# Early loads on ScalarE's queue, a shorter row scale and earlier quarter sums in a one-core hybrid decoder layer

## The chip, the core and the metric

The kernel runs on one core of a Trainium2 chip. The metric is device time in microseconds (us) of one execution. Three runs of the kernel before took 1051.25, 1051.29 and 1051.93 us; the median is 1051.29. The engines are TensorE (PE, with its weight loads as PEld), VectorE (DVE), ScalarE (ACT), GpSimd (POOL) and SyncE (SP), which issues all DMA transfers of the kernel before.

## The reference

One decoder layer on 512 rows of 1024 float32 numbers:

```python
u = rmsnorm(x, ln1_g)
proj = u @ w_in                       # q, k, v, pool_in, z, xbc, dt_raw, gate_pre
y_a = dilated_attention_mixer(q, k, v, rel_bias) @ w_a
y_b = pool_mixer(pool_in, pool_w, pool_scale) @ w_b
y_c = ssd_mixer(z, xbc, dt_raw, ...) @ w_c
gates = sigmoid(gate_pre + b_gate).reshape(b, s, 3, D)
merged = gates[:,:,0] * y_a + gates[:,:,1] * y_b + gates[:,:,2] * y_c
x = x + merged @ w_o
x = x + conv_ffn(rmsnorm(x, ln2_g), ...)
return rmsnorm(x, final_g)

def rmsnorm(x, g):
    return x * rsqrt(mean(x * x, axis=-1) + 1e-6) * g
```

The matrices are x (512 x 1024), w_in (1024 x 10,256), w_a, w_b, w_c, w_o, and the two of the feed-forward part, whose inner width is 2816.

## The kernel before

**Products.** Every float32 product is made of three fast ones. A weight matrix is cast to a high part (`wh`, by ACT, L191) and the rest is its low part (`wl` = raw - wh, by DVE, L211); activations have the same two parts (`uh`, `ul`). `mm3` (L224) adds wh x uh, then wh x ul, then wl x uh (in the order of its loop) into one PSUM bank, with k running over blocks of 128 rows of the inner dimension.

**Jobs and preparation.** The program is a list of jobs (`program`, L1395), each with a piece of weights of up to 1 MB. Ahead of job n the loop at L1581 prepares: the low part of job n+1 (with `job.then`, a difference of weights, behind it), the cast of job n+2 and the load of job n+3 (`prepare`, L1588). Then the body of job n issues its matmuls. Instructions stand on each engine in the order in which the program text issues them; each engine works them off in order, and waits for what an instruction needs.

**Steps.** Smaller work is written as generators. `step()` (L145) is called behind most chunks of matmuls; it issues the casts that were put off (`flush`), then lets every running item go on by one `yield`, in the order in which they were started, and starts one waiting item. `after(n, it)` (L160) lets n steps go by first.

**The start.** Four blocks of 128 rows of x are loaded as two halves of 128 x 512 each (`load_x`, L1457). SP issues block 0, the norm weights `g8`, the identity `eye`, block 1, then the weights of job 0 in two halves and of job 1 (`fetch`, L170), then blocks 2 and 3. PE meanwhile multiplies ones (`warm_up`). For blocks 0 and 1 the loop at L1526 makes the row scale r = 1/sqrt(mean + eps): squares of the two halves with their sums (`squares`, L429: ACT for the first half, DVE or ACT for the second), their sum (L1485), v (L417), a square root on ACT (L418), a reciprocal and one Newton step (L419 to L426). L1528 multiplies the identity by r into `diag`, and PE turns and scales the block in one product (`turn_scale`, L1523). Then ACT casts the weights of job 0 (L1534), and `turned` (L1491) multiplies by the norm weights `g1` and splits into uh (ACT, L1494) and ul (DVE, L1495). The first matmuls on them are at L1507. Ahead of all this ACT loads its table for the square root with a one-element operation on `warm` (L1450).

**The middle.** The v projections of attention groups 1 and 2 are one product of 1024 rows by 768 columns, made with seven quarter products instead of eight (`sevens`, L336, called by `v_pair`, L591). Its jobs come in the order A11, j=4, A12, j=1, j=2, j=3, A22. Those with a number use added or subtracted halves of u, which four items make ahead of time, one for each pair of k (`sums_of_u`, L395). An item takes four steps: A adds uh and ul to plain halves (L400, twice); B makes the sums and differences (L318 to L321); C casts them (ACT, L324, L325); D makes the low parts sal and sbl (DVE, L327, L328). The four items are started by a `Call` ahead of the fourth job of the w_b product:

```python
if i == 3:
    yield Call(lambda: running.extend(after(p + 1, sums_of_u(p)) for p in range(4)))
```

Between that place and the first of the seven jobs lie that job, of two columns of which the first (column 6) has a step in its middle (`chunk_a2`, L239, by `more`), and two gate jobs of two columns each, with a step behind each column. The evacuation of a gate column is a sigmoid on ACT (L1050) and a multiplication on DVE (L1052). Each of the seven jobs has 24 matmuls of 384 columns, 12 for each of two row blocks, and one step at its end; each row block has four with wh x the high parts, four with wh x the low parts, four with wl x the high parts.

**The end.** The last product adds into the rows block by block; behind each block the final norm (`norm_late`, L460) makes the second half of the row, then the first (L473, two operations), and SP stores them in this order (L1383).

Tiles of 128 x 512 come from one pool of 54 (`T`, L108).

Of the kernel before, what the change touches and what calls it, by code (L numbers as in the profile page):

```python
# [10 lines left out]
F32 = mybir.dt.float32  # L11
F32R = mybir.dt.float32r
AF = mybir.ActivationFunctionType
OP = mybir.AluOpType
AX = mybir.AxisListType

P = 128
S = 512
D = 1024
KD = D // P  # L20
EPS = 1e-6
# [62 lines left out]
def trunk(ctx: ExitStack, tc, out, x, rel_bias, ln1_g, w_in, b_gate, w_a, pool_w, pool_scale, w_b,  # L84
# [3 lines left out]
    act, dve, pool, pe, sp = nc.scalar, nc.vector, nc.gpsimd, nc.tensor, nc.sync  # L88

    x, w_in, w_a, w_b, w_c, w_o = x[0], w_in[0], w_a[0], w_b[0], w_c[0], w_o[0]  # L90
    w_up, w_down = ffn_w_up[0], ffn_w_down[0]
    out = out[0]

    cpool = ctx.enter_context(tc.tile_pool(name="const", bufs=1))
# [13 lines left out]
    def T(name, dt=F32, shape=(P, S)):  # L108
        return big.tile(list(shape), dt, name=name, tag="t")
# [7 lines left out]
    def small(name, shape, dt=F32):  # L117
        return tiny.tile(list(shape), dt, name=name, tag="tiny")

    eye = cpool.tile([P, P], F32, name="eye")  # L120
# [4 lines left out]
    waiting, running = [], []  # L125
    FREE = ()

    def fill(items):

        for it in items:  # L130
            at = next((i for i, w in enumerate(waiting) if w is FREE), None)
            if at is None:
                waiting.append(it)
            else:
                waiting[at] = it
# [24 lines left out]
    def after(n, it):  # L160
        for _ in range(n):
            yield
        yield from it
# [57 lines left out]
    def wsrc(w, k0, k1, c0, c1):  # L221
        return w[k0 * P:k1 * P, c0:c1].rearrange("(k p) c -> p k c", p=P)
# [91 lines left out]
    def sums_of(f0, f1, ah, al, found):  # L314


        sa, sb = T("sa"), T("sb")
        dve.tensor_tensor(sa[:, LO], f0[:, HI], f1[:, HI], OP.add)  # L318
        dve.tensor_tensor(sa[:, HI], sa[:, LO], f0[:, LO], OP.subtract)
        dve.tensor_tensor(sb[:, LO], f0[:, LO], f0[:, HI], OP.subtract)  # L320
        dve.tensor_tensor(sb[:, HI], f1[:, LO], sa[:, HI], OP.subtract)  # L321
        yield
        bh, bl = T("sbh", F32R), T("sbl", F32R)
        act.copy(ah, sa)  # L324
        act.copy(bh, sb)  # L325
        yield
        dve.tensor_sub(al, sa, ah.bitcast(F32))  # L327
        dve.tensor_sub(bl, sb, bh.bitcast(F32))  # L328
        for j, h, l, half in ((1, ah, al, LO), (2, ah, al, HI), (3, bh, bl, LO), (4, bh, bl, HI)):
            found(j, h[:, half], l[:, half])  # L330
# [64 lines left out]
    def sums_of_u(p):  # L395

        f = []
        for k in (2 * p, 2 * p + 1):
            f.append(T("uf"))
            dve.tensor_tensor(f[-1], uh[:, k, :].bitcast(F32), ul[:, k, :].bitcast(F32), OP.add)  # L400
        yield
        yield from sums_of(*f, T("sah", F32R), T("sal", F32R),
                           lambda j, h, l: US.__setitem__((j, p), (h, l)))
# [10 lines left out]
    def rstd_of(ss, cols, n):  # L414

        sq, v, r, t, r2 = (small(nme, [P, cols]) for nme in ("sq", "v", "r", "rt", "r2"))
        dve.tensor_scalar(v, ss, 1.0 / n, EPS, OP.mult, OP.add)  # L417
        act.activation(sq, v, AF.Sqrt)  # L418
        dve.reciprocal(r, sq)  # L419
        if cols == 1:  # L420
            dve.scalar_tensor_tensor(t, r, v, r, OP.mult, OP.mult)
        else:
            dve.tensor_mul(t, r, r)
            dve.tensor_mul(t, t, v)
        dve.tensor_scalar(t, t, -0.5, 1.5, OP.mult, OP.add)
        dve.tensor_mul(r2, t, r)  # L426
        return r2

    def squares(eng, src, ss):  # L429
        junk = T("junk")  # L430
        if eng is act:
            act.activation(junk, src, AF.Square, accum_out=ss)
        else:
            dve.scalar_tensor_tensor(junk, src, 1.0, src, OP.mult, OP.mult, accum_out=ss)
# [933 lines left out]
    def early(tb):  # L1368
        yield
        fin[tb] = norm_early(X1[tb, 0], fin["g"])  # L1370

    def blocks_of(h, acc, opened, keep):
        def evac(tb, ps):
            t = X1[tb, h]
            dve.tensor_tensor(t, t, ps, OP.add)
            if h == 0:
                running.append(early(tb))
                return
            v0, xg0 = fin[tb]
            for _ in norm_late(t, fin["g"], v0, lambda xg1: ((xg1, xg1), (xg0, xg0))):  # L1380
                xg1 = _
            for i, o in ((1, xg1), (0, xg0)):
                sp.dma_start(out[tb * P:(tb + 1) * P, i * S:(i + 1) * S], o)  # L1383

        return jobs_b(lambda k0, k1: [wsrc(w_down, KS + k0, KS + k1, h * S, h * S + S)], S,
                      lambda k, tb: ACTS[KS + k][0][:, tb * P:(tb + 1) * P],
                      lambda k, tb: ACTS[KS + k][1][:, tb * P:(tb + 1) * P], KF - KS, evac,
                      mk=(MM, SM)[h], tail=2 if h else 0, acc=acc, opened=opened, keep=keep)
# [6 lines left out]
    def program():  # L1395
        yield from jobs_a(w_in, C_POOL, 8, uhk, ulk, KD, pool_evac)
        yield Call(lambda: waiting.append(rows_of_bias()))
        yield from v_jobs(0)
        yield from qk_jobs(0)
        yield from pool_out_job()  # L1400
        yield Call(lambda: attend(0))
        yield Call(lambda: waiting.insert(3, ssd_prep()))
        for i, job in enumerate(branch_jobs(1, w_b, YB, 8, more=range(7))):
            if i == 3:
                yield Call(lambda: running.extend(after(p + 1, sums_of_u(p)) for p in range(4)))
            yield job
        load, pair = v_pair()
        yield Call(load)
        yield from gate_jobs(1, 0, SPLIT)
        yield from pair  # L1410
        yield from qk_jobs(1)
        yield Call(lambda: attend(1))
        yield from gate_jobs(1, SPLIT)
        yield from jobs_a(w_in, C_XBC, 12, uhk, ulk, KD, xbc_evac)
        yield Call(ssd_start)
        yield from qk_jobs(2)
        yield Call(lambda: attend(2))
        yield Call(lambda: fill([after(2, combine())]))
        yield from gate_jobs(0)
        many = {"a": branch_jobs(0, w_a, AO, 3), "g": gate_jobs(2),  # L1420
                "Z": z_jobs(0), "z": z_jobs(1)}
        for token in MIX:
            if token in many:
                yield next(many[token])
            else:
                yield Call(lambda i=int(token): waiting.append(y_norm(i)))
        yield Call(finish)
        yield from branch_jobs(2, w_c, YT, 8, last=True)
        yield Call(load_x1)
        for pair in range(2):  # L1430
            for h in range(2):
                yield from wo_jobs(pair, h)
            if pair == 0:
                yield Call(ff_cols)
        for i, job in enumerate(up_jobs()):
            yield job
            if i == 3:
                yield Call(put_x1)
        yield Call(lambda: fin.setdefault("g", grow(final_g)))
        yield Call(finish)  # L1440
        yield from down()

    jobs = list(program())
    weights = [j for j in jobs if isinstance(j, Job)]


    xin, warm = {}, small("warm", [P, 1])
    dve.memset(ones, 1.0)
    dve.memset(warm, 1.0)
    act.activation(warm, warm, AF.Sqrt)  # L1450
# [3 lines left out]
        for i in range(n):  # L1454
            pe.matmul(first[3][:, :P], ones, ones, start=True, stop=True)

    def load_x(tb):  # L1457
        for h in range(2):
            t = xin[tb, h] = T("xin")
            sp.dma_start(t, x[tb * P:(tb + 1) * P, h * S:(h + 1) * S])  # L1460

    load_x(0)
    g8, g1 = T("g8"), cpool.tile([P, KD], F32, name="g1")
    sp.dma_start(g8[:KD, :P], ln1_g[0].rearrange("(k p) -> k p", p=P))
    sp.dma_start(eye, c_eye)
    load_x(1)
    fetch(weights[0], 2)
    fetch(weights[1])
    load_x(2)
# [10 lines left out]
    def row_squares(tb, ss, n=1, eng=dve):  # L1480

        for i in range(n):
            squares(act, xin[tb + i, 0], ss[:, i:i + 1])
            squares(eng, xin[tb + i, 1], ss[:, n + i:n + i + 1])
        dve.tensor_tensor(ss[:, :n], ss[:, :n], ss[:, n:2 * n], OP.add)  # L1485
        return ss[:, :n]
# [30 lines left out]
    diag = [T("diag") for _ in range(2)]  # L1517
# [6 lines left out]
        pe.matmul(bank(k)[:, tb * P:(tb + 1) * P], x_block(tb, k), diag[tb][:, :P], start=True, stop=True)  # L1524

    for tb in range(2):  # L1526
        r = rstd_of(row_squares(tb, small("ss", [P, 2]), eng=(dve, act)[tb]), 1, D)
        dve.tensor_scalar(diag[tb][:, :P], eye, r, None, OP.mult)  # L1528
        if tb == 0:
            for k in range(KD):  # L1530
                turn_scale(0, k)
# [12 lines left out]
    ss = row_squares(2, small("ss", [P, 4]), 2)  # L1544
    next(parts)
    r = rstd_of(ss, 2, D)
    for tb in (2, 3):
        for h in range(2):
            t = xin[tb, h]
# [30 lines left out]
    n = 0  # L1580
# [66 lines left out]
```

## Time and profile before

| | us |
|---|---|
| runs (median, lowest, highest) | 1051.29, 1051.25, 1051.93 |
| profiled execution, its own time | 1052.9 |
| span of the profiled execution | 1050.8 |
| PE busy | 1037.0 |
| DVE busy | 642.9 |
| ACT busy | 467.4 |
| first matmul on uh (L1507) | 13.32 |
| first matmul of the job A11 | 209.55 |
| last matmul's result taken (L1375) | 1043.98 |
| last store issued | 1047.6 |

Times inside an execution count from the start of its span. A line of the profile's timeline gives start, length, engine, line of the code, operation and its tiles, and in brackets the idle time before and what ended it. The list of waits gives who waited for whom: total, times and longest. The chain is followed back from the last instruction, at each step to what released it. The table by windows gives, for each stretch, the busy time of the engines, the clock that TensorE was granted (1.00 is full), the share of the 16 DMA engines and the rate in GB/s. A busy PE can be a waiting one or a slow one in part, since matmuls are pipelined and the clock can be lower; so the granted clock is read beside it.

### The profile page before, as it was taken

The numbers are of one execution on the slowest core, as the hardware profiler recorded it, in microseconds if no ns is written. First come the engines' busy times: TensorE is split into PE (matmuls) and PEld (weight loads), VectorE is DVE, ScalarE is ACT, GpSimd is POOL, SyncE is SP. The second block draws the span as 40 slices with busy tenths as digits, with TensorE's granted clock in tenths as the row PEclk, the third lists the DMA queues.
The fourth block names the chain that finished last, engine by engine and source line by source line (L and its number), as shares of the span: only waits on it lengthen the run. The fifth ranks groups of instructions, "written<-read, shape, count | busy, mean of one in ns | idle before, by whom it ended". The sixth has DMA issues, their size and how long they took to land.

```text
span 1050.8 us, 13095 instructions
## 1 busy us (share of the span) xinstructions
PE 1037.0 (99%) x5220; PEld 864.9 (82%) x5220; DVE 642.9 (61%) x867; ACT 467.4 (44%) x753; POOL 137.7 (13%) x118
## 2 busy tenths in 40 slices
PE   8999999999999999999999999999999999999997
PEld 8888877898888887787887888898888888878885
DVE  5563565675356657576658856766766556556545
ACT  5432544343474363566554324545444443433331
POOL 1670000000000001100143500001111111110110
PEclk9999999999999999999999999999999999999999
DMA  7544312026322354641252426653232322362322
GB/s 241 156 125 136 113 49 74 31 56 182 104 80 81 80 149 112 151 121 52 79 147 85 150 91 220 205 161 119 81 119 82 107 94 82 119 240 67 114 100 80
DMA packets 119787, 121.80 MB, mean 116 GB/s; under 512 B 5523, under 2 KB 101590, under 8 KB 119727
## 3 DMA queue, kind: packets, MB, share of 16 engines
q1 hardware_dynamic: 119727, 120.98, 37.4%
q8 instruction: 41, 0.67, 0.3%
q14 instruction: 19, 0.16, 0.0%
HBM read 115.07 MB, written 4.32 MB: 114 GB/s over the span
## 4 chain that ended last, share of the span: by engine, by line
PE 94%; DVE 3%; DMA 1%; ACT 1%; issue 1%; POOL 0%; SPq 0%; DVEq 0%; ACTq 0%; POOLq 0%
PE pa L230 32%; PE pu L230 22%; PE pb L230 17%; PE pqk L230 9%; PE pa L1507 2%; PE p L230 2%; PE ps L656 1%; PE pu L1329 1%; PE po L695 1%; PE pt L683 1%; PE ppw L230 1%; DVE wl L211 1%; PE py L955 1%; DMA raw<-in_w_in_dram 1%; PE pyo L961 1%
## 5 line engine op out<-in xcount | busy, mean ns | idle before, releaser
L211 DVE TENSOR_TENSOR wl<-raw,wh 128x2048 fp32r<-128x2048 f32 (+3 forms) x95 | 218.6, 2302 | 80.3 <-ACT wh L191 42.3
L191 ACT CAST wh<-raw 128x1024 fp32r<-128x1024 f32 (+3 forms) x188 | 189.6, 1026 | 68.5 <-DVE raw L333 21.1
L230 PE MATMUL pa<-uh,wh 128*128 128x512 f32 x384 | 98.8, 399 | 0.0
L1165 DVE SCALAR_TENSOR_TENSOR hc<-pu,fcol,hc 128x510 f32<-128x510 f32 x88 | 65.9, 748 | 50.8 <-ACT hc L1162 49.2
L230 PE MATMUL pa<-uh,wl 128*128 128x512 f32 x384 | 95.0, 390 | 0.3 <-DVE wl L211 0.3
L230 PE MATMUL pa<-ul,wh 128*128 128x512 f32 x384 | 95.0, 390 | 0.0
L230 PEld LDWEIGHTS pa<-uh,wl 128*128 128x128 f32 x384 | 72.0, 188 | 15.6 <-DVE wl L211 0.7
L230 PEld LDWEIGHTS pa<-ul,wh 128*128 128x128 f32 x384 | 72.1, 188 | 15.2
L230 PE MATMUL pu<-uh,wh 128*128 128x512 f32 (+1 forms) x352 | 83.7, 380 | 0.0
L230 PE MATMUL pu<-uh,wl 128*128 128x512 f32 (+1 forms) x352 | 83.5, 380 | 0.0
L230 PE MATMUL pu<-ul,wh 128*128 128x512 f32 (+1 forms) x352 | 83.5, 380 | 0.0
L230 PEld LDWEIGHTS pa<-uh,wh 128*128 128x128 f32 x384 | 70.2, 188 | 15.2 <-issue 1.0
L230 PEld LDWEIGHTS pu<-uh,wh 128*128 128x128 f32 x352 | 64.1, 188 | 12.7 <-ACT uh L448 0.2
L230 PEld LDWEIGHTS pu<-ul,wh 128*128 128x128 f32 x352 | 64.2, 188 | 12.5
L230 PEld LDWEIGHTS pu<-uh,wl 128*128 128x128 f32 x352 | 64.2, 188 | 12.5
L1162 ACT ACTIVATE hc<-pu,fcol,fcol 128x512 f32<-128x512 f32 x40 | 31.2, 779 | 75.4 <-PE pu L230 75.2
L1170 POOL TENSOR_TENSOR hc<-hc 128x512 f32<-128x512 f32 x22 | 31.5, 1430 | 223.5 <-DVE hc L1165 169.3
L934 POOL TENSOR_TENSOR xd<-xc,dec 128x512 f32<-128x512 f32 x6 | 6.4, 1063 | 364.0 <-DVE xc L925 345.4
L677 ACT ACTIVATE sb<-sb,nm 128x128 f32<-128x128 f32 (+1 forms) x72 | 30.1, 419 | 22.9 <-DVE nm L674 17.2
L1050 ACT ACTIVATE sg<-pa,col 128x512 f32<-128x512 f32 x24 | 16.5, 687 | 51.8 <-PE pa L230 51.7
L230 PE MATMUL pqk<-uh,wh 128*128 128x512 f32 x144 | 36.9, 394 | 0.0
L230 PE MATMUL pqk<-ul,wh 128*128 128x512 f32 x144 | 36.3, 390 | 0.0
(343 smaller groups left out, 1752.4 us busy)
## 6 DMA issues: line engine op xcount, KB each, us to landing
raw<-in_w_in_dram SPq DMA_DIRECT2D x25, 1024.0 KB
raw<-in_ffn_w_up_dram SPq DMA_DIRECT2D x22, 1024.0 KB
raw<-in_w_in_dram SPq DMA_DIRECT2D x20, 512.0 KB
raw<-in_ffn_w_down_dram SPq DMA_DIRECT2D x10, 1024.0 KB
raw<-in_w_o_dram SPq DMA_DIRECT2D x8, 1024.0 KB
raw<-in_w_b_dram SPq DMA_DIRECT2D x4, 1024.0 KB
al<-ad SPq DMA_DIRECT2D x16, 256.0 KB
raw<-in_w_c_dram SPq DMA_DIRECT2D x4, 1024.0 KB
```

The costliest lines, as they stand in the source:

```text
L191: act.copy(job.high[:, :, o], job.raw[:, :, o])
L211: (eng or dve).tensor_tensor(l[:, :, o], job.raw[:, :, o], h[:, :, o].bitcast(F32), OP.subtract)
L230: pe.matmul(ps, l, r, start=first and n == 0, stop=last and n == total - 1)
L656: pe.matmul(pss[i][:, o:o + w * P], q[r, n * P:(n + 1) * P], k[r, kb * P:(kb + w) * P], start=True, stop=True)
L677: act.activation(sb[:, off:off + w * P], sb[:, off:off + w * P], AF.Exp, bias=nm[:, n, h:h + 1], accum_out=ls[:, n, h:h + 1])
L683: pe.transpose(pt[:, o:o + P], sb[:, o:o + P], eye)
L695: pe.matmul(po[DH * hh:DH * hh + DH, n * P:(n + 1) * P], V[g, kb + i][:, (2 * c + hh) * DH:(2 * c + hh + 1) * DH], probs[2 * c + hh, nb][: ...
L1050: act.activation(s, ps, AF.Sigmoid, bias=col[:, o:o + 1])
L1162: act.activation(t, ps, AF.Identity, bias=ff["c1"][:, ff["b"] + m:ff["b"] + m + 1], scale=fw(2, m))
L1165: dve.scalar_tensor_tensor(t[:, sh:], ps[:, :S - sh], fw(k, m), t[:, sh:], OP.mult, OP.add)
L1170: pool.tensor_tensor(a, a, t, OP.mult)
L1507: pe.matmul(first[2 * n + j][:, lo:hi], a[:, k, j * P:(j + 1) * P], b[:, k, lo:hi], start=a is wh and b is uh and k == 0, stop=a is wl and ...
```

## The change

There are four edits.

1. The loads of block 1 of x, of the identity and of the norm weights are issued by ACT, and stand at the head of ACT's program, before the operation on `warm`. SP's order is block 0, the weights of jobs 0 and 1, blocks 2 and 3.
2. The row scale of blocks 0 and 1 is written out in place: the two sums of squares have tiles of their own and go into v one after the other, and `diag` is the identity times r times the Newton factor rt in one operation, so that the product of the two is no longer made.
3. The four items of added halves wait p steps instead of p + 1.
4. Of the last row block (tb = 3) the first half of the row is stored by ACT instead of SP.

```diff
-                sp.dma_start(out[tb * P:(tb + 1) * P, i * S:(i + 1) * S], o)
+                (sp if i or tb < 3 else act).dma_start(out[tb * P:(tb + 1) * P, i * S:(i + 1) * S], o)
...
-                yield Call(lambda: running.extend(after(p + 1, sums_of_u(p)) for p in range(4)))
+                yield Call(lambda: running.extend(after(p, sums_of_u(p)) for p in range(4)))
...
+    def load_x(tb, eng=sp):
+        for h in range(2):
+            t = xin[tb, h] = T("xin")
+            eng.dma_start(t, x[tb * P:(tb + 1) * P, h * S:(h + 1) * S])
+
+    g8, g1 = T("g8"), cpool.tile([P, KD], F32, name="g1")
+    load_x(0)
+    load_x(1, act)
+    act.dma_start(eye, c_eye)
+    act.dma_start(g8[:KD, :P], ln1_g[0].rearrange("(k p) -> k p", p=P))
     dve.memset(ones, 1.0)
     dve.memset(warm, 1.0)
     act.activation(warm, warm, AF.Sqrt)
...
-    load_x(0)
-    g8, g1 = T("g8"), cpool.tile([P, KD], F32, name="g1")
-    sp.dma_start(g8[:KD, :P], ln1_g[0].rearrange("(k p) -> k p", p=P))
-    sp.dma_start(eye, c_eye)
-    load_x(1)
     fetch(weights[0], 2)
     fetch(weights[1])
     load_x(2)
...
-        r = rstd_of(row_squares(tb, small("ss", [P, 2]), eng=(dve, act)[tb]), 1, D)
-        dve.tensor_scalar(diag[tb][:, :P], eye, r, None, OP.mult)
+        s0, s1, v, sq, r, rt = (small(n, [P, 1]) for n in ("s0", "s1", "v", "sq", "r", "rt"))
+        squares(act, xin[tb, 0], s0)
+        squares((dve, act)[tb], xin[tb, 1], s1)
+        dve.tensor_scalar(v, s0, 1.0 / D, EPS, OP.mult, OP.add)
+        dve.scalar_tensor_tensor(v, s1, 1.0 / D, v, OP.mult, OP.add)
+        act.activation(sq, v, AF.Sqrt)
+        dve.reciprocal(r, sq)
+        dve.scalar_tensor_tensor(rt, r, v, r, OP.mult, OP.mult)
+        dve.tensor_scalar(rt, rt, -0.5, 1.5, OP.mult, OP.add)
+        dve.tensor_scalar(diag[tb][:, :P], eye, r, rt, OP.mult, OP.mult)
```

## The prediction

> **What bounds the kernel now.** First the page: busy shares and the slices with the granted clock.
>
> ```profile
> PE 1037.0 (99%) x5220; PEld 864.9 (82%) x5220; DVE 642.9 (61%) x867; ACT 467.4 (44%) x753; POOL 137.7 (13%) x118
> PEclk9999999999999999999999999999999999999999
> ```
>
> TensorE (PE) is busy 99% of the span. So a change can gain only where PE waits or runs at a lower clock: at the start, in the few waits that are left, and behind the last matmul. The list of PE's waits is the second view (total, times, longest in us); its other four lines sum to 2.3 us.
>
> ```profile
> PE uT L1524 <- DVE diag L1528: 2.2, 2, 1.5
> PE pb L230 <- DVE sbl L328: 2.2, 1, 2.2
> ```
>
> The change touches the first two and the tail. Third, the chain that ended last, in order of time, shows which of them is paid for.
>
> ```profile
> 3.88 7.94 DMA raw<-in_w_in_dram
> 11.87 0.93 issue
> 12.80 0.48 ACT uh L1494
> ...
> 214.37 1.67 DVE w L333
> 216.04 0.60 DVE sal L327
> 216.64 0.61 DVE sbl L328
> 217.25 0.04 issue
> 217.29 25.59 PE pb L230 x137
> ```
>
> At the start the chain runs not through diag (L1528) but through the transfer of the first weights: their second half is issued at 3.88 and lands at 11.82, ACT casts it, and only then comes uh. In the middle it leaves PE for 3.3 us of VectorE (DVE): a difference of weights (L333) and the two subtractions of the last halves (sal, sbl). The windows around that place (length; PE, PEld, DVE, ACT, POOL busy; granted clock; DMA share; GB/s) show a second loss.
>
> ```profile
> 213.56:217.29 3.73, 1.55 (x9) 1.23 (x8) 3.73 (x5) 1.94 (x3) 0.00 (x0) 1.00 0.00 0
> 217.80:221.00 3.20, 3.20 (x12) 3.20 (x11) 2.78 (x2) 0.48 (x1) 0.00 (x0) 0.50 0.00 0
> 221.75:225.90 4.15, 4.15 (x25) 4.15 (x25) 1.75 (x2) 3.42 (x5) 0.00 (x0) 1.00 0.00 0
> ```
>
> PE stands for 2.2 us, and behind that its clock is 0.50 from 217.8 to 221; the stretch behind that has 1.00 again.
>
> **The added halves one step sooner (the middle).** Each of four items takes four steps: A (two additions, L400), B (four half-wide operations, L318 to L321), C (two casts on ACT), D (two subtractions, L327 and L328). Item 3 has its D in the eighth step behind the line that starts them: three steps in the last job of w_b (column 6 of `more` has one in the middle), four in the two gate jobs, and the eighth behind the first of the seven jobs ("A11"). The second of the seven (j=4) reads sbl of all items. So D of item 3 is queued behind that job's low part (L211) and the difference W0 (L333). With after(p) it falls in the seventh step, ahead of both.
>
> Price of the stall: the 24 matmuls of job j=4 take from 213.56 to 221.75 (starts of weight loads) = 8.19 us; the next 24 of the same shape take 221.75 to 225.91 = 4.16. Difference 4.0 us: 2.2 of standing, 1.8 of half clock.
>
> Does DVE manage it? From 199.59 to 212.62 it has no pause: three multiplications of yo (L1052) 1.8, D 1.2, B 1.46, A 1.2, low part 1.8, difference 1.7, D 1.2, B 1.47, D 1.2: 13.0 us. One D, one B and one A (3.9 us) of these go a step ahead, where DVE has pauses of 4.17 us before 192.33 and 2.72 before 199.59 (behind 192.33 it then has 0.6 + 1.2 + 1.46 + 1.2 + 1.3 = 5.8 us, done at 198.1). In the new order 8.6 us follow 199.59, done at 208.2. Next is the multiplication that waits for ACT's sigmoid (209.75 + 0.69 = 210.44): 0.65 to 211.1, D of item 3 1.2 to 212.3, the low part 1.75 to 214.05. Job j=4 starts at 213.56 and needs sbl of item 3 at its eighth matmul (214.8) and the low part at its ninth (213.56 + 8 x 0.173 = 214.95). Both are there, the tighter by 0.9 us. What is late next: the low part for A12 ends at about 217.6 and is needed at 219.1. Later work hangs on PE's own progress, so it moves along. I take **-4.0**; bounds -2.2 (the half clock stays) and -4.1.
>
> A rule to weigh here: the Trainium skill (TensorE: Matmul & The Clock Gate, "Part 1: The HAM clock gate") gives half rate after at least one idle window of about 3.4 us. A stand of 2.2 us would not bring it by that, and the middle would then be worth 2.2; the rows show the half clock right behind 2.2 us.
>
> **Loads by ScalarE's queue (the start).** SP issues in this order now; each line is start and length, and the third has three transfers.
>
> ```profile
> 0.74 0.86 SPq L1460 DMA_DIRECT2D xin<-in_x_dram  x2
> 1.65 0.37 SPq L1464 DMA_DIRECT2D g<-in_ln_g_dram  x1
> 2.06 0.35 SPq L1465 DMA_DIRECT2D eye<-in_c_eye_dram  x1
> 2.46 0.90 SPq L1460 DMA_DIRECT2D xin<-in_x_dram  x2
> 3.40 4.83 SPq L179 DMA_DIRECT2D raw<-in_w_in_dram  x3
> ```
>
> Four issues leave SP, so the first weights are issued at 1.65 instead of 3.40. But until their second half lands, the same engines move the same bytes: 0.52 MB for each of two blocks, 1.05 MB of weights, 0.07 of identity and norm weights, 2.17 MB. They are at work from 2.0 on, with one dip (the last two columns are DMA share and GB/s):
>
> ```profile
> 2.00:3.50 1.50, 1.50 (x9) 1.50 (x8) 0.00 (x0) 0.22 (x2) 0.00 (x0) 1.00 0.94 303
> 3.50:4.50 1.00, 1.00 (x7) 1.00 (x6) 0.01 (x1) 0.65 (x2) 0.00 (x0) 1.00 0.83 179
> 4.50:8.00 3.50, 2.84 (x18) 2.65 (x18) 1.99 (x9) 1.00 (x4) 0.00 (x0) 1.00 0.92 284
> ```
>
> At about 300 GB/s the microsecond from 3.5 would move 0.30 MB and moved 0.18: 0.12 MB / 300 GB/s = 0.4 us. That is what an earlier issue can fill. I take **-0.4**; the bounds are -1.75 (the full 3.40 - 1.65) and +1.8 (below).
>
> What it adds: four issues on ACT ahead of its table load. No issue by ACT is in this trace; by SP's rows one takes 0.27 (a tiny one) to 3.69 us (the weights behind a full queue), and one of x at most 1.61. By the nearest rows, SP's own at an empty queue, it is 0.41 with the gap: ACT's load of 1.28 us then starts at 2.4 instead of 0.73 and its Sqrt of warm ends at 3.9, where ACT idles until 3.85 anyway. Cover: behind its last issue ACT needs table load 1.28, warm 0.2, squares 0.8, wait for v and Sqrt 0.85, two squares 1.65, Sqrt 0.6, two casts 2.0 = 7.4 us to uh. With uh at 12.4 the last issue may end at 4.9, 1.04 us each. At 1.61 each it ends at 7.2 and uh comes at 14.6: +1.8.
>
> Block 0 now shares the engines with block 1. Its halves landed at 3.85 and 4.49; both blocks together (1.05 MB at 300 GB/s from 2.0, and the lag of 1 to 2 us behind the bytes that x shows) land by 6.5 to 7.5, block 1 (8.29 before) sooner. Identity lands with them and is needed for diag. Then diag of block 0 is done near 8.1 (7.04 before) and diag of block 1 at 10.2 (10.77 before); the weights at 11.4 still come last. PE would stand from the end of its warm-up (6.43) to 8.2; its stand of 1.5 us before 10.83 left the clock at 1.00, that of 2.2 in the middle did not. At half clock the 16 turns of block 0 take 4.1 instead of 2.05 us, to 12.3, and uh comes at about 12.8, the whole gain of the start.
>
> **The scale.** For each block the product L426 (0.16) goes, and the sum L1485 becomes a second v operation of the same size: one operation less a block. In block 1 one v operation also runs before the second sum is ready. Off that chain go 0.19 + 0.2 = 0.4 us. It lies beside the transfer of the weights: **0**. Uncovered it would be a gain of 0.4.
>
> **The last store by ACT.** The last stores on SP:
>
> ```profile
> 1047.17 0.81 SPq L1383 DMA_DIRECT2D out_dram<-xg  x2
> ```
>
> The second issue starts at 1047.6, and DVE has the second half (L473, 1046.59 + 1.00) at 1047.59, so SP is not what it waits for: **0**, bounds -0.35 (one issue) and +0.45 (a dearer one on ACT).
>
> **Sum.** -4.0 - 0.4 = -4.4 us. The profiled execution took 1052.9 (span 1050.8 and 2.1 around it); it would take 1048.5. It lies 1.6 above the median of 1051.29, whose runs have no profile. On the median: **1046.9 us**. A measurement tells 0.2% (2.1 us) from no change.
>
> **Rivals.**
> - *The middle gives only part* (0.13): DVE is over 0.9 us later than worked out, or the half clock comes without the stand. For it: the margin is thin, and DVE's order is full. Against: the pauses ahead are 6.9 us for 3.9. -0.4 - 2.2: **1048.7**.
> - *The start gives nothing or loses* (0.16): the engines have the same 2.17 MB to move, at a share of 0.8 to 1.1 already, and PE's stand or ACT's issues may cost. -4.0 + 0 = **1047.3**; with issues of 1.61 us 1051.29 - 4.0 + 1.8 = **1049.1**. Beside it stands the Trainium skill (DMA: Bandwidth & Descriptors, "Issuing engines are not separate DMA queues"): transfers of all engines run on the same 16 DMA engines, and only time to issue is saved. By that rule it is 1047.3; the share in the rows agrees but for the dip.
> - *The stall only moves* (0.07): item 3 is in time, but its operations push a low part past its need, and PE stands as long at A12 or at j=1. Against: margins of 1.5 and 1.4 us there. Only the start's 0.4 is left: **1050.9**.
> - *Slower* (0.04): ACT's four issues hold its table load. With 3.69 us each the last ends at 15.5 and uh comes at 22.9, +10.1; less 4.0: **1057.4**. It decides from 2.7 us an issue, where the start loses 6.1. Against: the 3.69 was behind a full queue.
>
> The forecast has 0.60, on its own 1045.3 to 1047.8. The range: down to 1045.3 (start -1.75, middle -4.1, end -0.1), up to 1049.2, the first two rivals within. Below 1049.2 lies faster: 0.60 + 0.13 + 0.16 = 0.89, of which 0.01 goes to the same: 0.88; same 0.08; slower 0.04.
>
> **What would show it.** Right: no wait of PE for sbl, the job j=4 in about 4.2 us, clock 1.00 through it; first weights landed near 11.4 and uh near 12.4; ACT's first square before 4.6; the tail as long as now. Wrong: a wait of PE for wl between 213 and 226, a clock of 0.5 there without a stand, uh later than 12.8, or issues on ACT over 1 us.

## The result, and the profile after

| | before | after |
|---|---|---|
| median of 20 runs each (us) | 1051.21 | 1049.24 |
| lowest, highest | 1048.74, 1053.35 | 1046.47, 1051.41 |
| profiled execution, its span | 1052.9, 1050.8 | 1049.47, 1047.4 |
| first square of block 0's second half (L434) | 4.49 | 6.42 |
| `diag` of block 0, of block 1 | 6.75, 10.49 | 8.29, 9.95 |
| first matmul on uh (L1507 before, L1508 after) | 13.32 | 14.18 |

The ratio is 0.998, with a 95% interval of 0.9972 to 0.9988: 1.3 to 2.9 us faster. That is a little under half of the forecast gain of 4.4 us. 1049.24 lies just above the upper end of the range (1049.2), and the gain lies on the 0.2% that a measurement tells from no change, with the interval on both sides of it. The two profiled executions differ by 3.4 us, more than the medians; so what follows is read from places inside the executions, each over several of them.

First the list of PE's waits in the kernel after (total, times, longest; all of it).

```profile
PE uT L1525 <- DVE v L1531: 2.2, 1, 2.2
PE pa L1466 <- DVE relb L511: 1.1, 1, 1.1
PE pb L230 <- DVE wl L211: 0.5, 1, 0.5
PE pu L230 <- ACT uh L448: 0.2, 1, 0.2
```

The wait for sbl (2.2 us) is gone. A wait of the same length has come at the start, for the turning of block 0. The line names v, but that is the v of block 1, the next operation on DVE (8.55 to 8.70). What PE needed is `diag`, to which the weight load of the same products is put down, and the chain, in order of time, runs through it (first the weight load from the timeline, then the chain):

```profile
8.69 2.42 PEld L1525 LDWEIGHTS uT<-diag,xin 128*128 128x128 f32 x16 [2.45 <-DVE diag L1537]
```

```profile
1.19 5.21 DMA xin<-in_x_dram
6.40 0.02 issue
6.42 0.70 DVE junk L434 x2
...
8.29 0.35 DVE diag L1537
8.64 0.07 DVE v L1531
8.71 2.69 PE uT L1525 x16
11.40 0.20 PE pa L1541
11.61 2.81 PE uT L1525 x16
14.42 9.59 PE pa L1508 x80
```

The chain starts with a transfer of x that lands at 6.40, the second half of block 0, and no longer with the weights. Then it runs through the scale, `diag`, and the turns of both blocks. Each 16 turns take 2.7 to 2.9 us; in the kernel before they took 2.05. The windows (length; PE, PEld, DVE, ACT, POOL busy; granted clock; DMA share; GB/s) tell why, and what the transfers did:

```profile
2.00:3.50 1.50, 1.50 (x9) 1.50 (x8) 0.00 (x0) 0.61 (x1) 0.00 (x0) 1.00 0.90 195
3.50:4.50 1.00, 1.00 (x7) 1.00 (x6) 0.00 (x0) 0.87 (x2) 0.00 (x0) 1.00 0.83 238
4.50:8.00 3.50, 2.04 (x10) 1.74 (x9) 1.24 (x6) 1.31 (x4) 0.00 (x0) 1.00 1.10 333
...
10.00:12.70 2.70, 2.70 (x13) 2.45 (x13) 0.46 (x2) 1.25 (x2) 2.42 (x2) 0.50 1.09 347
213.00:217.80 4.80, 4.80 (x30) 4.80 (x29) 4.59 (x4) 2.52 (x5) 0.00 (x0) 1.00 0.00 0
217.80:221.00 3.20, 3.20 (x20) 3.20 (x20) 2.47 (x3) 2.15 (x4) 0.00 (x0) 1.00 0.00 0
```

Behind the stand at the start the clock is 0.50 from 10.0 to 12.7; in windows of 0.1 us the half clock reaches from 9.9 to 13.3, which is 3.4 us. In the middle it is 1.00 throughout, without a stand. From 2.0 to 8.0 the engines move 0.29 + 0.24 + 1.17 = 1.70 MB, against 0.45 + 0.18 + 0.99 = 1.62 MB in the profiled execution before: hardly more. What changed is which bytes go first. The timeline (start, length, engine; in brackets the idle time before and what ended it):

```profile
0.74 0.90 ACTq L1452 DMA_DIRECT2D xin<-in_x_dram  x2
0.74 0.87 SPq L1452 DMA_DIRECT2D xin<-in_x_dram  x2
1.66 5.09 SPq L179 DMA_DIRECT2D raw<-in_w_in_dram  x3
1.66 0.45 ACTq L1457 DMA_DIRECT2D eye<-in_c_eye_dram  x1
2.15 0.71 ACTq L1458 DMA_DIRECT2D g<-in_ln_g_dram  x1
2.89 1.28 ACT L1461 ACT_TABLE_LOAD   x1 [2.89 <-issue]
...
6.42 0.69 DVE L434 SCALAR_TENSOR_TENSOR junk<-xin 128x512 f32<-128x512 f32 x1 [5.39 <-DMA xin<-in_x_dram]
...
10.67 1.04 ACT L191 CAST wh<-raw 128x1024 fp32r<-128x1024 f32 x1 [0.47 <-DMA raw<-in_w_in_dram]
```

Block 1 is issued by ACT at the same time as block 0 by SP, and the weights follow at 1.66. ACT's four issues take 0.41 to 0.71 us each, and its table load ends at 4.17, ahead of the first data. The second half of the weights is taken at 10.67, which is earlier than before (11.85). ACT still waited 0.47 us for it, but the first matmul no longer does.

**Where the time went, by places.** Two matmuls that every kernel has cut the execution into stretches: the first at L656 (attention scores) and the first at L955. The middle lies between them, the start ahead of them.

| | before | after | difference |
|---|---|---|---|
| start to first L656 | 126.2 | 127.0 | +0.8 |
| first L656 to first L955 | 274.3 | 270.3 | -4.0 |
| last L1375 to the end of the span | 6.8 | 6.9 | +0.1 |

The rest (L955 to the last L1375) takes 642.2 to 644.4 us in all executions of all kernels below. It varies without regard to the edits, and it is why one execution, or a difference of two spans, doesn't settle a gain of 2 us.

### The profile page after: what moved, and what is told of

Same layout as the page of the kernel before. It is cut to its first block, busy times and chain, and to the rows that moved or that the text cites. A ratio compares the mean times of both kernels' runs of the same rounds, so it can differ in the third digit from the quotient of the medians.

```text
span 1047.4 us, 13090 instructions
## 1 busy us (share of the span) xinstructions
PE 1036.3 (99%) x5220; PEld 864.5 (83%) x5220; DVE 642.6 (61%) x865; ACT 467.6 (45%) x753; POOL 138.0 (13%) x118
## 4 chain that ended last, share of the span: by engine, by line
PE 92%; DVE 3%; DMA 2%; ACT 2%; issue 0%; DVEq 0%; SPq 0%; ACTq 0%
PE pa L230 35%; PE pu L230 22%; PE pb L230 13%; PE pqk L230 9%; PE pa L1508 2%; PE p L230 2%; DVE wl L211 2%; PE ps L656 1%; PE po L695 1%; PE pt L683 1%; DMA raw<-in_ffn_w_up_dram 1%; PE ppw L230 1%; ACT wh L191 1%; PE py L955 1%; DMA raw<-in_w_o_dram 1%; PE pyo L961 1%
## 5 line engine op out<-in xcount | busy, mean ns | idle before, releaser
L230 PEld LDWEIGHTS pu<-uh,wh 128*128 128x128 f32 x352 | 64.1, 188 | 12.8 <-ACT uh L448 0.4
```

Source lines behind the costliest of these rows:

```text
L230: pe.matmul(ps, l, r, start=first and n == 0, stop=last and n == total - 1)
```

## The experiments

**The order of arrival** is the theory. The middle gives its whole 4.0 us. The start loses 1.6 us of that, because one queue on SP delivered in the order of need (block 0, identity, block 1, weights), while two queues share the same engines: block 0 lands late, PE stands for over 2 us and then turns at half clock. It has three rivals. **The clock:** in the middle the half clock comes by chance or anyway, only the stand of 2.2 us is gained, and the start is neutral. **The issues:** ACT's four issues hold its table load and its squares. **The small edits:** the short scale or the last store costs something.

The expectations are quoted as they were recorded ahead of each run. Where letters stand in them for the theories of that moment, the numbers beside the letters are what the run is held against. The times came above what was expected by 0.4 to 0.5 us in e3, e6, e7, e8 and e9, and by 1.7 us in e10; the first matmul on uh came later than expected in e5, e7, e9 and e10.

The starts of all kernels in one table, so that each run can be looked up: DVE's square of block 0's second half; `diag` of block 0 and of block 1; ACT's cast of the second half of the weights ("ready": it did not wait for the transfer); first matmul on uh; first L656; whether the clock was 0.50 in the turns.

| kernel | square | diag 0 | diag 1 | weights | on uh | L656 | half clock |
|---|---|---|---|---|---|---|---|
| before | 4.49 | 6.75 | 10.49 | 11.85 | 13.32 | 126.2 | no |
| b0_before_again | 4.39 | 6.65 | 8.87 | 10.26 | 11.73 | 124.7 | no |
| e1_sums_alone | 4.54 | 6.8 | 9.3 | 10.63 | 12.10 | 125.0 | no |
| e12_sums_again | 4.50 | 6.77 | 9.34 | 10.83 | 12.30 | 125.2 | no |
| e8_no_act_loads | 4.13 | 6.00 | 8.95 | 11.24 | 12.71 | 125.6 | no |
| e6_block_1_on_sp | 4.75 | 6.62 | 8.28 | 10.29 | 11.76 | 124.7 | no |
| after | 6.42 | 8.29 | 9.95 | 10.67 | 14.18 | 127.0 | yes |
| e2_start_alone | 5.75 | 8.12 | 9.70 | ready | 14.01 | 126.8 | yes |
| e11_changed_again | 5.63 | 7.92 | 9.50 | ready | 13.80 | 126.6 | yes |
| e3_longer_warm_up | 5.71 | 8.48 | 10.06 | ready | 12.82 | 125.6 | no |
| e5_identity_first | 4.64 | 6.51 | 10.54 | ready | 14.30 | 127.2 | yes |
| e7_identity_first_filled | 4.64 | 6.51 | 11.04 | ready | 13.25 | 126.0 | no |
| e9_both_blocks_on_act | 6.41 | 8.28 | 11.89 | ready | 15.32 | 128.1 | yes |
| e10_halves_over_both_queues | 4.94 | 6.82 | 9.37 | 12.13 | 13.61 | 126.5 | no |

### The change taken apart

**The kernel before once more** has no edit.

> The kernel before, unchanged, for the clock of each of its executions. Its profiled execution has 1.6 us of lost clock behind the stand for sbl (half clock from 217.8 to 221.2) and about 1.6 behind the last matmul: 0.997. Theory C (the half clock behind a stand of about 2 us comes in some executions only, and for lengths that differ): the mean clock spreads over 0.995 to 0.999 and the time follows it, near 1 us for 0.001. Rival S (it comes in each execution alike): all at 0.997, and the times spread for another reason.

Measured: 1050.97 us, ratio 1.0001 (0.9993 to 1.001). The middle stretch is 274.3 us again. The wait and the window around it (columns as above) are those of the first execution:

```profile
PE pb L230 <- DVE sbl L328: 2.2, 1, 2.2
```

```profile
217.20:220.50 3.30, 3.30 (x12) 3.30 (x11) 1.82 (x2) 0.21 (x1) 0.00 (x0) 0.50 0.00 0
```

So the half clock behind the stand in the middle is no accident of one execution. But it does not come in every one. Each run has its mean granted clock on record, and the traces tell how to read it. Every stretch of half clock in them lasts 3.4 us (6.8 in e9), and each 3.4 us take 0.0016 off the mean; behind the last matmul every trace loses some more. The seven traces with such a stretch at the start or in the middle have means of 0.995 to 0.997, the seven without one 0.998 or 0.999. All runs sorted by that (number of runs, mean time):

| kernel | 0.997 or less | 0.998 or more |
|---|---|---|
| before (b0 and the runs beside the experiments) | 48, 1051.8 us | 46, 1050.4 us |
| after (result and e11) | 21, 1049.6 us | 11, 1047.7 us |
| halves alone (e1, e12) | 1, 1049.1 us | 13, 1047.4 us |
| longer warm-up (e3) | none | 12, 1048.4 us |

By this the half clock in the middle came in about half of the runs of the kernel before, and the one at the start in two of three runs of the changed kernel; the runs with it are 1.4 and 1.9 us longer. That is theory C of the expectation, and not rival S, which wanted 0.997 in all. It is read from rounded means: these runs have no trace of the stretch itself, and the twelve of b0 alone show the link of clock and time only faintly.

The start differs between the two executions as well. Chain and timeline of this run:

```profile
3.88 6.36 DMA raw<-in_w_in_dram
10.24 0.02 issue
```

```profile
10.26 1.04 ACT L191 CAST wh<-raw 128x1024 fp32r<-128x1024 f32 x1 [0.76 <-DMA raw<-in_w_in_dram]
```

With the same program the second half of the weights landed at 10.24 instead of 11.82. The prediction had taken 11.82 as a property of the kernel; it is one draw of a time that varies by 1.6 us (five executions with these loads: 10.24, 10.6, 10.8, 11.2, 11.8).

**Only the added halves** (kernel before with one edit):

```diff
-  running.extend(after(p + 1, sums_of_u(p)) for p in range(4))
+  running.extend(after(p, sums_of_u(p)) for p in range(4))
```

> Only the added halves one step sooner. Both theories: no wait of PE for sbl, job j=4 in 4.2 us, and the start as before (first matmul on uh at 13.3). Theory C: the gain is the stand of 2.2 us in each execution and 1.8 of half clock in some of them: 2.2 to 4.0 us, near 3, and a mean clock of 0.998 to 0.999 with little spread. Rival S: 4.0 us.

Measured: 1047.47 us, ratio 0.9969 (0.9957 to 0.998). The middle stretch is 270.3 us (125.0 to 395.3), 4.0 less than in all three traced executions with the late halves, and no wait for sbl is left. The half clock goes with the stand; had it come anyway, only 2.2 would be gained, and that half of the rival falls. The other half, that it comes by chance, holds by the clocks above: the three traces had it, and in a run without it only the stand of 2.2 us is there to gain. Over all runs that makes about 3.1 us (an estimate: 2.2 and half of 1.8). The ratio, 3.3 us with an interval of 2.1 to 4.5, does not tell this from 4.0.

**Only the start** (kernel after, with the halves and the store put back):

```diff
-  running.extend(after(p, sums_of_u(p)) for p in range(4))
+  running.extend(after(p + 1, sums_of_u(p)) for p in range(4))
...
-  (sp if i or tb < 3 else act).dma_start(out[...], o)
+  sp.dma_start(out[...], o)
```

> Only the start: loads by ACT's queue and the shorter scale; halves and last store as before. Theory C: block 0 lands 1.9 us later because block 1 shares the engines, PE stands about 2.2 us behind its warm-up, and half clock comes behind that in most executions: slower by 0.7 us (as in the profiled execution of the changed kernel) to 3, near 1. Rival S: slower by 0.7, alike in all. Rival Q (the loss is one of ACT's queue, such as the later table load): PE's first stand is not what decides, and the time stays the same when the stand is filled.

Measured: 1053.05 us, ratio 1.0021 (1.0011 to 1.0032). By itself the new start costs 1.2 to 3.4 us. Middle stretch 274.3, as before. Its chain and its window at the start:

```profile
1.66 6.35 DMA eye<-in_c_eye_dram
...
8.12 0.35 DVE diag L1537
```

```profile
10.00:12.00 2.00, 2.00 (x9) 1.75 (x9) 0.21 (x2) 1.00 (x1) 1.96 (x1) 0.50 1.09 349
```

Here the last to come was the identity: issued at 1.66 behind block 1 in ACT's queue, landed at 8.02. In the kernel after it was block 0's second half. Both are the same displacement: something that was early in one queue now stands beside or behind half a megabyte of block 1. The half clock is there too.

**The changed kernel with a longer warm-up** (`WARM = 12` to `WARM = 16`, eight matmuls of ones more), to shorten PE's stand.

> The changed kernel with 16 instead of 12 warm-up products, so that PE works until about 8.3 us and stands 0.4 instead of 2.15 before diag. Theory C: the clock stays at 1.00 to 14 us, turns of block 0 in 2.05 us, first matmul on uh at 12.4 to 12.9 instead of 14.2, the mean clock 0.998 to 0.999, and 1.3 to 3 us faster than the changed kernel: 1046.2 to 1048. Rival Q: no gain over the changed kernel (1049.2).

Measured: 1048.37 us, ratio 0.9977 (0.9969 to 0.9985). The eight matmuls made the warm-up only 0.45 us longer (it ends at 6.99 instead of 6.54), so the stand of 0.4 us that was expected did not come. Here `diag` was later still, since it waited for the identity until 8.48, but PE stood for 1.89 us instead of 2.15 and the clock stayed at 1.00 (timeline, then window):

```profile
8.48 0.35 DVE L1537 TENSOR_SCALAR diag<-eye,r,rt 128x128 f32<-128x128 f32 x1 [0.93 <-DMA eye<-in_c_eye_dram]
8.88 2.05 PE L1525 MATMUL uT<-diag,xin 128*128 128x128 f32 x16 [1.89 <-DVE v L1531]
...
12.82 0.72 PE L1508 MATMUL pa<-uh,wh 128*128 128x256 f32 x4
```

```profile
10.00:12.00 2.00, 2.00 (x18) 1.86 (x17) 0.54 (x3) 1.50 (x3) 1.60 (x1) 1.00 1.09 349
```

18 matmuls in the window where e2 has 9. The first matmul on uh comes at 12.82 instead of 13.8 to 14.2. So the loss of the start has two parts: about 1.2 us by the half clock, and about 0.4 us by the late `diag` itself (12.82 against a mean of 12.43 of the five executions with all loads on SP). The times of e3 and after overlap, so the split rests on the traces; the mean clocks agree with it (no run of e3 at 0.997 or less, 21 of the 32 of the changed kernel).

### Which load must come first

**The identity ahead of block 1 on ACT's queue:**

```diff
-  load_x(1, act)
   act.dma_start(eye, c_eye)
   act.dma_start(g8[:KD, :P], ...)
+  load_x(1, act)
```

> The changed kernel, with ACT issuing identity and norm weights ahead of block 1. Theory L (the loads on a second queue share the engines with block 0, and identity comes behind block 1): identity no longer holds diag, but block 0's second half still lands at 5.5 to 6.5 instead of 4.4, so diag of block 0 is done at 7.6 to 8.6, PE stands 1.2 to 2.2 us; a part of the loss stays: first matmul on uh at 12.5 to 14, time 1048 to 1049. Rival I (identity alone is late): diag at 7.0, first matmul at 11.7 to 12.1 as with the loads of before, 1047. Rival A (ACT's late table load holds the first square): first square not before 4.4, and no change against the changed kernel.

Measured: 1048.76 us, ratio 0.9981 (0.9971 to 0.999). Block 0 and the identity are on time again (`diag` at 6.51), but block 1 is not:

```profile
4.64 0.69 DVE L434 SCALAR_TENSOR_TENSOR junk<-xin 128x512 f32<-128x512 f32 x1 [3.61 <-DMA xin<-in_x_dram]
...
7.69 0.63 ACT L432 ACTIVATE junk<-xin 128x512 f32<-128x512 f32 x1 [1.85 <-DMA xin<-in_x_dram]
...
8.72 0.63 ACT L432 ACTIVATE junk<-xin 128x512 f32<-128x512 f32 x1 [0.30 <-DMA xin<-in_x_dram]
```

Its halves, now beside the weights, land at 7.7 and 8.7; in b0 both were squared by 7.3. PE stands twice (1.4 and 1.8 us), the turns of block 1 run at half clock in this trace, and nothing is won: the stand has moved from block 0 to block 1. By the mean clocks only two of the eleven runs, this one among them, had the half clock.

**The same with a still longer warm-up** (`WARM = 21`).

> As the run with identity first, and 21 warm-up products instead of 12, so that PE works until about 8.2 us. Theory L with the clock: no half clock at the start, turns of both blocks at full rate; first matmul on uh at 11.7 to 12.8, time 1047 to 1048. It tells the share of the half clock (about 1 to 1.4 us against the run with identity first, if that has it) from the share of the late block.

Measured: 1048.4 us, ratio 0.9975 (0.9966 to 0.9985).

```profile
9.22 0.63 ACT L432 ACTIVATE junk<-xin 128x512 f32<-128x512 f32 x1 [1.06 <-DMA xin<-in_x_dram]
...
11.44 2.05 PE L1525 MATMUL uT<-diag,xin 128*128 128x128 f32 x16 [2.02 <-DVE diag L1537]
```

The late block remains (9.2 here), PE stands for 2.02 us, but the clock is not halved: the first matmul on uh comes at 13.25 instead of 14.30, L656 at 126.0 instead of 127.2. Again about 1.1 us for the half clock, between these two traces; the medians differ by 0.4, as few runs of e5 had it.

**Only the two small loads on ACT,** block 1 on SP behind block 0:

```diff
-  load_x(1, act)
   act.dma_start(eye, c_eye)
   act.dma_start(g8[:KD, :P], ...)
+  load_x(1)
```

> The changed kernel with only identity and norm weights on ACT's queue; block 1 goes back to SP behind block 0. Theory L: block 0 lands at 3.8 and 4.5 as before, diag of block 0 at 7.0, clock 1.00 at the start, first matmul on uh at 11.4 to 12.1, time as with the halves alone or a little less: 1046.7 to 1047.5. Rival A: the table load still comes late (two issues ahead of it), first square at 4 instead of 3.8, loss of 0.2 at most. If neither block nor identity was the cause, it stays at 1049.

Measured: 1047.96 us, ratio 0.9973 (0.9962 to 0.9984).

```profile
4.75 0.69 DVE L434 SCALAR_TENSOR_TENSOR junk<-xin 128x512 f32<-128x512 f32 x1 [3.72 <-DMA xin<-in_x_dram]
...
10.29 1.04 ACT L191 CAST wh<-raw 128x1024 fp32r<-128x1024 f32 x1 [0.76 <-DMA raw<-in_w_in_dram]
...
11.76 0.87 PE L1508 MATMUL pa<-uh,wh 128*128 128x256 f32 x4 [0.55 <-ACT uh L1495]
```

The order of need is back, and so is the start of b0, without half clock: the cast of the weights and the turns of block 1 both end at 11.2 to 11.3, and uh follows them. ACT issues loads here as well, so no cost of the second queue by itself is seen. It is the large transfer in it that costs.

**All loads as before, the other three edits kept:**

> The changed kernel with all loads back on SP as before: halves, scale and last store stay changed. All theories: 1047.0 to 1047.8, as with the halves alone (1047.5), since the shorter scale lies beside the landing of the weights and the last store is not what SP waits for. If the shorter scale gains: diag of block 1 0.4 us earlier, and the first matmul on uh still follows the weights (10.2 to 11.8 plus 1.5).

Measured: 1048.29 us, ratio 0.9972 (0.996 to 0.9983). It has the short scale and the store by ACT, and cannot be told from the halves alone (0.9969 and 0.9967); nothing that can be measured is left for the small edits. The short scale is seen where nothing hides it: from the square of the second half to `diag` of block 0 takes 1.87 us here (4.13 to 6.00), and 2.26 in b0 (4.39 to 6.65). The 0.4 us vanish behind the weights, which come at 11.24.

### Is it the sharing, or ACT?

**Both blocks on ACT, SP begins with the weights:**

```diff
-  load_x(0)
-  load_x(1, act)
+  load_x(0, act)
   act.dma_start(eye, c_eye)
   act.dma_start(g8[:KD, :P], ...)
+  load_x(1, act)
```

> The changed kernel with block 0 too on ACT's queue: ACT issues block 0, identity, norm weights, block 1; SP begins with the first weights. Theory L in its wider form (two queues share the engines, so whatever stands alone in its queue arrives early and pushes back what is needed first): block 0 now shares with the weights. Its second half lands later than 4.4, at 5.5 to 6.5, block 1 at 8 to 9.5, the weights at 8 to 9; diag of block 1 at 10.5 to 11.5, PE stands, first matmul on uh at 12.5 to 14; 1049 to 1050. Rival O (only a block behind identity or a block next to a block is late, the order on the queue decides): as with the loads of before, first matmul at 11.7 to 12.2, 1047.5.

Measured: 1050.4 us, ratio 0.9991 (0.9983 to 1.0).

```profile
6.41 0.69 DVE L434 SCALAR_TENSOR_TENSOR junk<-xin 128x512 f32<-128x512 f32 x1 [5.38 <-DMA xin<-in_x_dram]
...
10.07 0.63 ACT L432 ACTIVATE junk<-xin 128x512 f32<-128x512 f32 x1 [0.43 <-DMA xin<-in_x_dram]
```

Block 0 is first in its queue, and it is as late as in the kernel after (6.41 against 6.42). There it shared with block 1, here with the weights. The stand is 3.16 us, and the half clock lasts 6.8 us (7.7 to 14.5), twice as long as in the other traces, over the turns of both blocks. This is the slowest start, and nearly all of the middle's gain is spent.

**Halves over both queues, in the order of need:** of each of the two blocks and of the first weights the first half is issued by SP and the second by ACT.

```diff
-  eng.dma_start(t, x[...])
+  (act if h and tb < 2 else sp).dma_start(t, x[...])
...
-  sp.dma_start(raw[...], src[...])
+  (act if cuts > 1 and i else sp).dma_start(raw[...], src[...])
```

> The changed kernel with each early load split over both queues in the order of need: SP block 0 first half, block 1 first half, weights first half; ACT block 0 second half, identity, block 1 second half, norm weights, weights second half. Theory L: both queues hold the same order, so nothing overtakes: block 0 at 3.8 to 4.6, block 1 by 7, weights by 10.3; diag of block 0 at 7.0, of block 1 at 8.5 to 9, first matmul on uh at 11 to 12, the half clock gone: 1046.7 to 1048. Rival Q (a second queue costs by itself): 1049 like the changed kernel.

Measured: 1049.66 us, ratio 0.9985 (0.9977 to 0.9994).

```profile
12.13 1.04 ACT L191 CAST wh<-raw 128x1024 fp32r<-128x1024 f32 x1 [2.21 <-DMA raw<-in_w_in_dram]
...
13.61 0.87 PE L1508 MATMUL pa<-uh,wh 128*128 128x256 f32 x4 [1.78 <-ACT uh L1495]
```

Blocks and identity are near their old times (`diag` at 6.82 and 9.37). But the second half of the weights comes at 12.1, the latest of all: on ACT's queue it now has the weights of job 1 beside it, which in one queue stood behind it. This was not foreseen in that size. It fits the same mechanism, but was not tested apart.

**The changed kernel, and the halves alone, once more:**

> The changed kernel once more beside the next run, for a second trace of its start. Theory L: diag of block 0 at 8.1 to 8.9, PE's stand 1.9 to 2.3 us, first matmul on uh at 12.8 to 14.3; the length of the half clock differs from one execution to the other; 1049.2.

> Only the added halves one step sooner, once more beside the changed kernel. Theory L: 1047.5, 1 to 2 us faster than the changed kernel, with the first matmul on uh at 11.7 to 13.3.

Measured: 1048.47 us, ratio 0.9977 (0.9966 to 0.9988), and 1047.23 us, ratio 0.9967 (0.9955 to 0.9979). Half clock and a first matmul at 13.80 in the one, 12.30 and full clock in the other. The halves alone are the fastest of all kernels tried, by about 1 to 2 us ahead of the whole change; e6 and e8 lie within their interval.

## Why the prediction was wrong by half

**What bounds the kernel: right.** The stand and the half clock in the middle came in all three traced executions with the late halves (before, b0, e2), though by the mean clocks the half clock is missing in about half of the runs. The start's bound, the weights, was right in kind but too firm: 11.82 was the latest of five landings, and in e12 the chain runs through block 1 and its turns instead, which end within 0.1 us of the weights' cast.

**The middle: right in the traces, in size and in detail.** Forecast -4.0, measured -4.05 (274.3 to 270.2 or 270.3, in all eleven traced executions with the earlier halves). On a median the term was too large, by about 0.9 us by the estimate above: it counted the half clock in full, from one trace, and by the mean clocks only about half of the runs had it. The details can be read off the timeline of the kernel after, which is 0.76 us later than before at this place because of its start:

```profile
211.23 0.69 DVE L1052 TENSOR_TENSOR yo<-yo,sg 128x512 f32<-128x512 f32 x1 [2.25 <-ACT sg L1050]
...
212.44 0.68 DVE L328 TENSOR_TENSOR sbl<-sb,sbh 128x512 fp32r<-128x512 f32 x1
...
213.05 1.75 DVE L211 TENSOR_TENSOR wl<-w,wh 128x1536 fp32r<-128x1536 f32 x1
...
215.71 0.71 PEld L230 LDWEIGHTS pb<-wl,sbh 128*128 128x128 f32 x4
```

sbl of item 3 is done at 213.12 (forecast 212.3 + 0.76 = 213.06), the low part at 214.80 (214.05 + 0.76 = 214.81), and PE wants it at 215.71: the margin of 0.9 us that was worked out. The rivals "the middle gives only part" and "the stall only moves" had this margin as their point, and it held. The rule of the Trainium skill that was weighed there (TensorE: Matmul & The Clock Gate, "Part 1: The HAM clock gate"), about 3.4 us of idling for half rate, would have left the middle at 2.2. The traces differ from it: a stand of 2.2 us was followed by 0.50 in three of three, and without the stand it was gone. That it comes in only about half of the runs was not in the prediction.

**The start: this step failed.** It said that "the weights at 11.4 still come last", and hung the sum on them (-0.4). The weights did come earlier: against a mean landing of 10.94 in the five executions with all loads on SP by 0.3 us in the kernel after, and by 1 or more in e2 and e11, where ACT casts both halves in a row from 8.94 and 8.73. But the chain had left them: it now ran through block 0 or the identity, `diag`, and the turns of both blocks. Mean time of the first matmul on uh: 12.43 in those five executions, 14.00 in the three with the changed loads: **+1.6** (+1.5 at L656). With the middle that makes -4.05 + 1.6 = -2.45, inside the measured -1.3 to -2.9. Weighted by the mean clocks it is -3.1 for the middle and +1.2 for the start (two of three runs with 1.6, one with the 0.4 of e3), -1.9 in all; that is an estimate, and the medians (-2.0, and -3.1 beside e11) do not tell the two sums apart. The repeat e11, at 1048.47, lies inside the forecast range. On which side of its edge the number falls is chance; the step failed all the same.

Five things in the working of that step were not followed to the end.
- It had block 0 sharing the engines, and `diag` of block 0 done at 8.1 (8.64 came, and 8.26 to 8.83 in e2, e3 and e11). It took that as harmless, because the weights were later.
- It had PE's stand of 1.8 us and the half clock behind it, as a thing that could take "the whole gain of the start". It priced it by comparing 12.8 with the weights' path. In fact the half clock ran into the turns of block 1 too: not 4.1 us for block 0 and full speed behind it, but 3.4 us of half clock over both.
- It let uh come half a us behind the turns of block 0, and left out the turns of block 1. They stand ahead of the first matmul on PE, and uh needs them, since its first operands are 256 columns wide, both blocks. In the kernel after, ACT's first uh did come at 12.80, but PE was in the turns of block 1 until the first matmul began at 14.18.
- It measured that against one landing. With the mean landing of the weights (10.9) as measure, uh would have come at 11.9 by the old path, and the loss would have shown.
- It counted bytes, and those are the same; but it did not ask whose bytes come first. For the queue the sum matters, for the chain the order.

The rival "the start gives nothing or loses" was the right one. Its two prices were 0 and +1.8, and +1.6 is nearly the second; but the second was worked out from dear issues by ACT. Issues cost 0.41 to 0.71 us, as the row of SP had said, and did not decide (e6 issues by ACT too and shows no loss). What agrees with the runs is a sentence of the Trainium skill (DMA: Bandwidth & Descriptors, "Queues, rings and completion order"): each DMA engine takes turns between the queues that have work for it. Then a transfer at the head of its queue still gets only its share. The rows show that: block 0's second half is taken at 4.1 to 4.75 us where it follows the first on SP and ACT's queue begins with the small loads or has none, and at 5.6 to 6.4 where block 1 or the weights stood beside it from the start (4.94 in e10, where its two halves run on two queues).

**The scale and the last store: right at 0.** The scale is 0.4 us shorter and hidden (e8). The tail takes 6.9 us against 6.8; ACT issued the store in 0.37 us:

```profile
1044.19 0.37 ACTq L1383 DMA_DIRECT2D out_dram<-xg  x1
```

**Still open** is what decides whether the half clock comes behind a stand: see the last section.

## What to carry to other kernels

A second queue adds no bandwidth where the DMA engines are busy at a share of 0.8 to 1.1; what it changes is the order of arrival. So large loads that are needed one after the other belong in one queue, in the order of need, and only small ones beside them. Price a stand of PE of about 2 us at its length plus the half clock that can follow it, here 1.2 to 1.8 us more where it came. Whether it comes in each run is read from the clocks of many runs, not from one trace. And take the landing time of a transfer from several executions before a step is called hidden behind it.

## What the hardware did that was not expected

- **Half clock behind short stands.** In the middle a stand of 2.2 us brought 0.50 in three of three traces, and by the mean clocks in about half of the runs. At the start single stands of 2.06 (e2), 2.15 (after, e11) and 3.16 us (e9) brought it in their traces, and those of 1.78 (e10), 1.89 (e3) and 2.02 (e7) did not; shorter ones (0.3 to 1.5) never. In e5 1.82 us brought it, 4 us behind a first stand of 1.42, but by the mean clocks in two of eleven runs only. So no one length of a stand parts them.
- **The half clock has one length.** It lasted 3.4 us in seven of eight stretches and 6.8 in e9, and where PE worked on, the clock was 1.00 again behind it. It does not start with the stand: from the stand's end it took 0.1 us in e5, 0.5 in the middle of before and 1.2 to 1.4 at the start of after and in b0, and in e9 it began 1.0 us ahead of the end. What sets this time, and whether idle time is summed, was not tested.
- **The same loads land at different times.** The second half of the first weights landed between 10.24 and 11.82 us in five executions with the same loads, though the queue and its order are the same.
- **ACT's table load** takes 1.28 us wherever it stands. In the kernel after it was ready ahead of the data, though it came 2.2 us later (2.89 instead of 0.73). In e3, e5, e7, e9 and e10 ACT's first square follows it without a wait for data (at 4.16 to 5.68), but DVE's square of the second half ended later in each, so the load was not what `diag` waited for.
